# The upper parts of the weights, rounded by a second DMA from DRAM instead of by ScalarE

## The chip, the cores and the metric

One core of a Trainium2 chip runs the whole kernel. The metric is the time of one execution on the device in microseconds. Before the change it is 1176.87 us in the median of three runs (1175.96 to 1178.97).

## What is computed

One layer of a decoder for 512 prompt tokens and 8 sample tokens (520 columns in all), width 1024, float32. Cut to what matters here:

```python
z = rms_norm(x) @ w_in                       # 1024 -> q | k | v | g | gMLP u | gMLP v | a_ret | a_gm
o, new_state = retention(q, k, v, state)     # 4 heads, key 256, value 512; 8 samples with their own states
A = (silu(g) * head_rms(o)) @ w_ret_o
B = (gelu(u) * (tril(W_s) @ layer_norm(gelu(v)) + b)) @ w_gm_o
h = x + (sigmoid(a_ret) * A + sigmoid(a_gm) * B) @ w_o
h = h + (silu(f_gate) * f_up) @ w_ffn_down   # f_gate, f_up = rms_norm(h) @ w_ffn_in, hidden 2816
y = rms_norm(h)
```

The states of the samples (8 samples, 4 heads, 512 KB each) are read, updated and written back.

## The kernel before, in words

Activations lie with features on the partitions and tokens in the free dimension. A product of float32 quality is made of three products in float32r, a shorter float type: every operand is split into an upper part (the value rounded to float32r) and a lower part (what the rounding leaves), and `product` (L99 to L108) adds upper x upper, upper x lower and lower x upper for each 128x128 weight tile and each half of the 520 tokens. A block of weights is eight such tiles, [128, 1024] or 512 KB: 48 matmuls with 260 columns. There are 178 blocks: 80 of `w_in`, 16 of `w_ret_o`, 8 of `w_gm_o`, 8 of `w_o`, 44 of `w_ffn_in` and 24 of `w_ffn_down` (eight of these have six tiles).

`weights` (L84 to L97) brings a block in. SP issues the load of the raw block (L95), ScalarE casts it into the upper part `whi`, and VectorE subtracts (raw - `whi`) into the lower part `wlo`; both are in `split` (L79 and L82). Three raw buffers and two each of `whi` and `wlo` go round. The first two blocks come in pieces (`cuts`), and the three blocks of the last output tile go into big buffers of their own (`keep`: `khi`, `klo`).

The order of the stages is: the first activations and their split; four heads, each with q, k, v and gate products, the scores, the outputs, and eight samples; then the gMLP branch, the merge, the hidden layer and the output with its norm. Within a head `sample` loads a state S (three buffers, SP, L433), gets a broadcast of q and k from DRAM for every two samples (`qkb`, POOL, L436), has ScalarE make the key-value products (L442), updates S on VectorE (L443), stores it (`out_rss`, POOL, L444) and reads it out on VectorE (L447). At the end of a head come its row sums (`stats`, L511 and after) and the gated output (`gated`, L520), which are worked off in the next head's time and feed `gate_out`.

POOL also makes the rotary sums (L275, L276), the gate products (L515, L602), the layer norm's scale and shift (L595, L596) and the product in the hidden layer (L721).

Every engine works through its own queue in order, and so do the DMA issues in the queues of SP and POOL. That order is not written out by hand: a planner simulates the program and puts each instruction into its engine's queue when its inputs and a buffer are free in the simulation; semaphores hold the order on the chip.

Of the kernel before, what the change touches and what calls it, by code (L numbers as in the profile page):

```python
# [13 lines left out]
P = 128  # L14
D = 1024          # model width
KT = D // P       # contraction tiles of the model width
NP = 512          # prompt tokens
NS = 8            # sample tokens
T = NP + NS       # all tokens, in the free dimension
HT = T // 2       # tokens of one matmul  # L20
H = 4             # retention heads
DK = 256
DV = 512
NC = 4            # chunks of 128 prompt tokens
G = 4             # gMLP groups
NF = 2816 // P    # feature tiles of the hidden layer
PAST = 4096
EPS = 1e-6

NBIG = 26         # [128, 2, 520] buffers that all phases share  # L30
NFP = 4           # more of them, once the first phases' own buffers are free
NTMP = 5          # [128, 520] buffers for what lives shortly
NWARM = 16        # matmuls before the first operands
NSP = 6           # tiles of the first activations that GpSimd squares

# [6 lines left out]
def step_kernel(ctx: ExitStack, tc: tile.TileContext, io):  # L42
# [10 lines left out]

# [1 line left out]
    def ttile(name):  # L55
# [20 lines left out]
    def split(hi, lo, src, hi_eng=None, lo_eng=None):  # L76
        """src = hi + lo exactly, both with 12 significant bits."""
        if hi_eng is None:
            nc.scalar.copy(out=hi, in_=src)  # L79
        else:  # L80
            hi_eng.tensor_copy(out=hi, in_=src)
        (lo_eng or nc.vector).tensor_tensor(out=lo, in0=src, in1=hi.bitcast(F32), op=ALU.subtract)  # L82

    def weights(src, n, cuts=(), keep=False):  # L84
        """A block of n 128x128 weight tiles, split into two parts (in pieces, where it must start early)."""
        raw = wp.tile([P, 8 * P], F32, name="wraw", tag="wraw", bufs=3)
        if keep:
            hi, lo = flat(wide("khi", F32R)), flat(wide("klo", F32R))
        else:
            hi = wp.tile([P, 8 * P], F32R, name="whi", tag="whi")  # L90
            lo = wp.tile([P, 8 * P], F32R, name="wlo", tag="wlo")
        at = [0, *cuts, n]
        for a, b in zip(at, at[1:]):
            sl = slice(a * P, b * P)
            nc.sync.dma_start(out=raw[:, sl], in_=src[:, sl])  # L95
            split(hi[:, sl], lo[:, sl], raw[:, sl])
        return hi, lo  # L97

    def product(ps, w, at, x, first, last, fs=(0, 1)):  # L99
        """ps += w[:, at].T @ x, as hi*hi + hi*lo + lo*hi."""  # L100
        sl = slice(at * P, (at + 1) * P)
        wh, wl = w[0][:, sl], w[1][:, sl]
        for n, (a, k) in enumerate(((wh, 0), (wh, 1), (wl, 0))):
            for f in fs:
                nc.tensor.matmul(  # L105
                    (ps[f] if isinstance(ps, list) else ps[:, f])[:, 0:HT], a, x[:, k, f * HT : (f + 1) * HT],
                    start=first and n == 0, stop=last and n == 2,
                )  # L108

    def small_rsqrt(v, n, parts=P):  # L110
        """v ** -0.5 of a few positive columns: a bit-level guess and Newton's steps."""
        i0 = small.tile([P, 16], I32, name="rs_i0")[:parts, 0:n]
# [14 lines left out]
    def rsqrt_table(after):  # L127
        """Has ScalarE load the table of the roots ahead of their time, but after this."""
        one = small.tile([P, 1], F32, name="one", bufs=1)
        nc.scalar.activation(out=one, in_=after[:, 0:1], func=AF.Abs_reciprocal_sqrt)  # L130

    def newton_rstd(out, ps, scale, n):
        """(ps * scale + eps) ** -0.5"""
        y, v, t = (stile(f"rr_{x}")[:, 0:n] for x in "yvt")
        nc.vector.tensor_scalar(out=v, in0=ps, scalar1=scale, scalar2=EPS, op0=ALU.mult, op1=ALU.add)
        nc.scalar.activation(out=y, in_=v, func=AF.Abs_reciprocal_sqrt)
        nc.vector.scalar_tensor_tensor(out=t, in0=y, scalar=-0.5, in1=y, op0=ALU.mult, op1=ALU.mult)
        nc.vector.tensor_tensor(out=t, in0=t, in1=v, op=ALU.mult)
        nc.vector.scalar_tensor_tensor(out=out, in0=t, scalar=1.5, in1=y, op0=ALU.add, op1=ALU.mult)

    def row_rstd(out, ps, width):
        """The same of sums over features, all tokens."""
        y, v, t = (stile(f"rr_{x}") for x in "yvt")
# [11 lines left out]
    def add_square(acc, src, first, pool=False, add=None):  # L155
        """acc (+)= src ** 2, the sums over features on their way."""
        q = acc if first else stile("sqr")
# [7 lines left out]
    def row_sums(acc):  # L165
        """Sums over the partitions, in all partitions, in two banks."""
        pr = [stile(f"sq{x}", F32R) for x in "hl"]
# [11 lines left out]
    def scaled_split(pr, src, g):  # L179
        """src * g (per partition) in two parts."""  # L180
        nc.scalar.activation(out=pr[:, 0, :], in_=src, func=AF.Copy, scale=g)
# [3 lines left out]

# [1 line left out]
    ones_r = const.tile([P, P], F32R, name="ones_r")  # L187
# [30 lines left out]

    # keeps TensorE's clock up until the first operands are there
    warm = ttile("warm")[:, 0:HT].bitcast(F32R)  # L220
# [29 lines left out]

    br = []           # what becomes the merge: retention branch, two feature tiles each

# [1 line left out]
    def unscaled(base, name):  # L254
        """The first two tiles, before the norm's scale is known."""
        raw = wide(f"{name}raw")
# [5 lines left out]
    def rotated(base, name, raw=None):  # L262
        """Rotary on two feature tiles (one head): float32 [P, 2, T]."""
        def turns(i, src):
# [14 lines left out]
    def gate_out(h, gated):  # L279
        """This head's part of the retention branch's output projection."""  # L280
        for m2 in range(KT // 2):
# [13 lines left out]
    def head(h, prev, dec):  # L295
# [24 lines left out]

        # keys by token, with the decay to the end of the prompt
        kth, ktl = wide("kth", F32R), wide("ktl", F32R)
# [21 lines left out]

        # scores, transposed: [s, t >= s]; rows of 512, 384 | 256 + 128
        sch = wide("sch", F32R), wide("sch2", F32R)
# [18 lines left out]

        # values by token
        vt = [wide(f"vt{i}", F32R) for i in range(4)]  # (hi, lo) x two chunks each
        vs = small.tile([P, NC, NS], F32, name="vs", bufs=2)

# [27 lines left out]

        # the samples' queries and keys, broadcast over the partitions by way of DRAM
        ps = aux("ps_qk")
# [14 lines left out]

        # swish gate
        gts = []
# [9 lines left out]

        # the samples: new states and what is read of them, values over the partitions
        os_ = small.tile([P, NC, NS], F32, name="os_", bufs=2)
# [22 lines left out]

        # the output by feature
        of = [wide("of0"), wide("of1")]
# [12 lines left out]

        # the state after the prompt
        def last_state():
# [33 lines left out]

        # the head norm and the gate, for the next head's time
        class Gating:
# [27 lines left out]

# [1 line left out]
    def sig_gate(m, name, out):  # L534
        """out = sigmoid of a merge gate, one feature tile."""
        pa = z_tile(m, name)
# [3 lines left out]
    def gmlp(gp):  # L540
# [40 lines left out]

        # layer norm over the features, by token
        def layer_norm(v, parts):
# [19 lines left out]

        # what the values of a chunk mix to, by feature
        mixed = [wide(f"mix{i}") for i in range(KT // 2)]
# [50 lines left out]

# [1 line left out]
    sg = [wide(f"sg{i}") for i in range(KT // 2)]  # L658
# [33 lines left out]

# [1 line left out]
    def ffn_tile(m, name):  # L694
# [9 lines left out]
    for i in range(NF):  # L704
        a, b = ttile("fa"), ttile("fb")
        pg = ev(ffn_tile(i, "ps_fg"))
        if i == 0:
            # the norm's scale isn't known yet
            nc.scalar.copy(out=halves(a), in_=pg)
# [16 lines left out]
    def down_weights(i, keep=False):  # L726
        """The three blocks of a tile of the output projection: (weights, first tile, tiles)."""
        for k0 in range(0, NF, 8):
# [8 lines left out]
    rsqrt_table(a)  # L737
    # the residual sum, times the last norm's gain
    hn = []
# [8 lines left out]

    # the last feature tile, half of the tokens after half of them
    i = KT - 1  # L750
# [97 lines left out]
```

## Time and profile before

| what | before |
|---|---|
| median of three runs | 1176.87 us |
| span of the profiled execution (its first to its last instruction) | 1173.5 us |
| TensorE matmul busy | 1146.2 us, 98% |
| VectorE busy | 682.5 us, 58% |
| ScalarE busy | 435.6 us, 37% |
| GpSimd busy | 231.5 us, 20% |
| moved by DMA | 148.49 MB, mean 127 GB/s |

The profile is of one execution. PE is TensorE's matmul, PEld its weight load, DVE is VectorE, ACT ScalarE, POOL GpSimd; SP only issues DMAs. A q behind an engine's name is its instruction queue. Issuing a DMA does not count as busy. A row with an arrow names the tile written and the tiles read. Waits are inferred: "A <- B: 3.6, 1, 3.6" is A idle for 3.6 us in total, once, 3.6 us at the longest, until B.

### The profile page before, as it was taken

The numbers are of one execution on the slowest core, as the hardware profiler recorded it, in microseconds if no ns is written. First come the engines' busy times: TensorE is split into PE (matmuls) and PEld (weight loads), VectorE is DVE, ScalarE is ACT, GpSimd is POOL, SyncE is SP. The second block draws the span as 40 slices with busy tenths as digits, with TensorE's granted clock in tenths as the row PEclk, the third lists the DMA queues.
The fourth block names the chain that finished last, engine by engine and source line by source line (L and its number), as shares of the span: only waits on it lengthen the run. The fifth ranks groups of instructions, "written<-read, shape, count | busy, mean of one in ns | idle before, by whom it ended". The sixth has DMA issues, their size and how long they took to land.

```text
span 1173.5 us, 21664 instructions
## 1 busy us (share of the span) xinstructions
PE 1146.2 (98%) x9240; PEld 1128.9 (96%) x9240; DVE 682.5 (58%) x1063; ACT 435.6 (37%) x672; POOL 231.5 (20%) x183
## 2 busy tenths in 40 slices
PE   8999999999999999998999999999999999999995
PEld 7999999999999998998999999999999999999995
DVE  7788747874896588449744336445445454532233
ACT  4355355532644365223233333333222222232220
POOL 7213201310141013007522012211101010101101
PEclk9999999999999999999799999999999999999998
DMA  7267337632753284221123222522222323223322
GB/s 268 88 216 282 105 114 251 233 121 90 268 200 127 90 295 168 78 91 55 58 73 100 96 90 94 160 91 90 90 91 90 102 82 105 86 87 99 83 80 73
DMA packets 45056, 148.49 MB, mean 127 GB/s; under 512 B 5240, under 2 KB 7688, under 8 KB 44960
## 3 DMA queue, kind: packets, MB, share of 16 engines
q1 hardware_dynamic: 37280, 119.74, 31.3%
q0 software_dynamic: 7680, 27.38, 6.2%
q8 instruction: 72, 1.18, 0.4%
q14 instruction: 24, 0.20, 0.1%
HBM read 125.99 MB, written 21.10 MB: 125 GB/s over the span
## 4 chain that ended last, share of the span: by engine, by line
PE 76%; DVE 12%; DMA 4%; issue 3%; ACT 3%; POOL 0%; DVEq 0%; ACTq 0%; POOLq 0%; SPq 0%
PE ps_fu L105 11%; PE ps_fg L105 11%; PE ps_fd L105 10%; PE ps_ro L105 8%; PE ps_v L105 5%; PE ps_gm L105 4%; PE ps_gu L105 4%; PE ps_ag L105 4%; PE ps_wo L105 4%; PE ps_gv L105 4%; DVE wlo L82 2%; DMA S<-in_st 2%; PE ps_g L105 2%; PE k L105 2%; PE ps_ar L105 2%
## 5 line engine op out<-in xcount | busy, mean ns | idle before, releaser
L79 ACT CAST whi<-wraw 128x1024 fp32r<-128x1024 f32 (+2 forms) x180 | 184.9, 1027 | 475.0 <-issue 96.5
L82 DVE TENSOR_TENSOR wlo<-wraw,whi 128x1024 fp32r<-128x1024 f32 (+2 forms) x180 | 256.9, 1428 | 97.0 <-ACT whi L79 92.3
L105 PE MATMUL ps_fu<-hg,whi 128*128 128x260 f32 x704 | 113.3, 283 | 0.0
L105 PE MATMUL ps_fg<-hg,whi 128*128 128x260 f32 x704 | 113.3, 283 | 0.0
L105 PE MATMUL ps_fd<-act,whi 128*128 128x260 f32 x616 | 98.7, 282 | 0.0
L105 PEld LDWEIGHTS ps_fu<-hg,whi 128*128 128x128 f32 x704 | 96.6, 189 | 0.0
L105 PEld LDWEIGHTS ps_fg<-hg,whi 128*128 128x128 f32 x704 | 96.6, 188 | 0.0
L105 PEld LDWEIGHTS ps_fd<-act,whi 128*128 128x128 f32 x616 | 84.3, 188 | 0.0
L105 PE MATMUL ps_g<-xg,whi 128*128 128x260 f32 x512 | 82.7, 283 | 0.0
L105 PE MATMUL ps_ro<-gated,whi 128*128 128x260 f32 x512 | 82.3, 282 | 0.0
L105 PE MATMUL ps_v<-xg,whi 128*128 128x260 f32 x512 | 82.2, 282 | 0.0
L721 POOL TENSOR_TENSOR fa<-fa,fb 128x520 f32<-128x520 f32 x22 | 28.7, 1304 | 229.1 <-ACT whi L79 194.2
L105 PEld LDWEIGHTS ps_ro<-gated,whi 128*128 128x128 f32 x512 | 70.6, 188 | 0.5
L105 PE MATMUL ps_fg<-hg,wlo 128*128 128x260 f32 x352 | 70.7, 282 | 0.0
L105 PE MATMUL ps_fu<-hg,wlo 128*128 128x260 f32 x352 | 70.7, 282 | 0.0
L105 PEld LDWEIGHTS ps_v<-xg,whi 128*128 128x128 f32 x512 | 70.1, 188 | 0.0
L105 PEld LDWEIGHTS ps_g<-xg,whi 128*128 128x128 f32 x512 | 69.9, 188 | 0.0
L442 ACT ACTIVATE kv<-qkb,vs 128x256 f32<-128x256 f32 x128 | 54.0, 498 | 26.7 <-DMA qkb<-qks 22.5
L105 PE MATMUL ps_fd<-act,wlo 128*128 128x260 f32 x308 | 61.9, 282 | 0.0
L720 DVE TENSOR_TENSOR fb<-ps_fu,rstd 128x520 f32<-128x520 f32 x21 | 14.7, 700 | 76.8 <-PE ps_fu L105 76.8
L163 POOL TENSOR_TENSOR sq<-sq,sqr 128x520 f32<-128x520 f32 x19 | 33.0, 1734 | 132.7 <-ACT sqr L161 128.4
L447 DVE SCALAR_TENSOR_TENSOR junk<-S,qkb 128x256 f32<-128x256 f32 x128 | 53.9, 421 | 2.3
(245 smaller groups left out, 2552.3 us busy)
## 6 DMA issues: line engine op xcount, KB each, us to landing
wraw<-in_w_in SPq DMA_DIRECT2D x78, 512.0 KB, 3.5
wraw<-in_w_ffn_in SPq DMA_DIRECT2D x44, 512.0 KB, 3.5
S<-in_st SPq DMA_DIRECT2D x32, 512.0 KB, 4.6
out_rss<-S POOLq DMA_DIRECT2D x32, 512.0 KB, 5.1
qkb<-qks POOLq DMA_DIRECT2D x16, 512.0 KB, 5.0
wraw<-in_w_ret_o SPq DMA_DIRECT2D x16, 512.0 KB, 3.5
wraw<-in_w_ffn_down SPq DMA_DIRECT2D x16, 512.0 KB, 3.5
wraw<-in_w_gm_o SPq DMA_DIRECT2D x8, 512.0 KB, 3.5
```

The lines of the kernel that those rows point to most:

```text
L79: nc.scalar.copy(out=hi, in_=src)
L82: (lo_eng or nc.vector).tensor_tensor(out=lo, in0=src, in1=hi.bitcast(F32), op=ALU.subtract)
L105: nc.tensor.matmul((ps[f] if isinstance(ps, list) else ps[:, f])[:, 0:HT], a, x[:, k, f * HT : (f + 1) * HT], start=first and n == 0, stop ...
L163: (add or nc.gpsimd).tensor_tensor(out=acc, in0=acc, in1=q, op=ALU.add)
L442: nc.scalar.activation(out=kv[:, j, :], in_=kb, func=AF.Copy, scale=vs[:, j, b : b + 1])
L447: nc.vector.scalar_tensor_tensor(out=junk, in0=S[:, j, :], scalar=1.0, in1=qb, op0=ALU.mult, op1=ALU.mult, accum_out=os_[:, j, b : b + 1],)
L720: nc.vector.tensor_tensor(out=halves(b), in0=pu, in1=halves(rstd), op=ALU.mult)
L721: nc.gpsimd.tensor_tensor(out=a, in0=a, in1=b, op=ALU.mult)
```

## The change

`weights` loads a block twice. POOL issues a DMA from DRAM straight into `whi`, whose type is float32r, so that the transfer rounds; SP loads the raw block as before; VectorE subtracts as before. ScalarE's cast is gone, save in the two blocks with `cuts`. The raw buffers become two, the buffers of `whi` three; `wlo` keeps two.

```diff
     def weights(src, n, cuts=(), keep=False):
-        raw = wp.tile([P, 8 * P], F32, name="wraw", tag="wraw", bufs=3)
+        raw = wp.tile([P, 8 * P], F32, name="wraw", tag="wraw", bufs=2)
         if keep:
             hi, lo = flat(wide("khi", F32R)), flat(wide("klo", F32R))
         else:
-            hi = wp.tile([P, 8 * P], F32R, name="whi", tag="whi")
+            hi = wp.tile([P, 8 * P], F32R, name="whi", tag="whi", bufs=3)
             lo = wp.tile([P, 8 * P], F32R, name="wlo", tag="wlo")
         at = [0, *cuts, n]
         for a, b in zip(at, at[1:]):
             sl = slice(a * P, b * P)
+            if cuts:
+                nc.sync.dma_start(out=raw[:, sl], in_=src[:, sl])
+                split(hi[:, sl], lo[:, sl], raw[:, sl])
+                continue
+
+            nc.gpsimd.dma_start(out=hi[:, sl], in_=src[:, sl])
             nc.sync.dma_start(out=raw[:, sl], in_=src[:, sl])
-            split(hi[:, sl], lo[:, sl], raw[:, sl])
+            nc.vector.tensor_tensor(out=lo[:, sl], in0=raw[:, sl], in1=hi[:, sl].bitcast(F32), op=ALU.subtract)
         return hi, lo
```

The rest of the diff takes comments out.

## Rows read from the trace of the kernel before

**Rows 1.** The page: the span, then busy us, share and instructions of each engine.
```profile
span 1173.5 us, 21664 instructions
...
PE 1146.2 (98%) x9240; PEld 1128.9 (96%) x9240; DVE 682.5 (58%) x1063; ACT 435.6 (37%) x672; POOL 231.5 (20%) x183
```

**Rows 2.** TensorE's waits: us in total, times, longest.
```profile
PE ps_ar L105 <- DVE mv L588: 3.6, 1, 3.6
...
PE ps_mix L620 <- DVE gvl L82: 1.8, 1, 1.8
PE ps_ss L173 <- ACT sqh L79: 1.6, 1, 1.6
...
PE ps_ar L105 <- DVE ve L590: 1.4, 1, 1.4
...
PE ps_v L105 <- DVE wlo L82: 0.7, 2, 0.4
```

**Rows 3.** Windows: first and last head's sample stretch; busy us, count, clock, DMA share.
```profile
72.00:104.00 32.00, 32.00 (x233) 30.40 (x232) 26.65 (x73) 20.30 (x40) 5.34 (x10) 1.00 0.88 307
...
409.00:441.00 32.00, 32.00 (x238) 30.70 (x238) 26.62 (x75) 19.77 (x39) 5.35 (x10) 1.00 0.82 293
```

**Rows 4.** Chain of waits, second and fourth head: start us, us, what.
```profile
195.19 5.74 DMA out_rss<-S
...
200.99 8.36 DMA S<-in_st
...
237.63 2.44 DVE gt L520 x4
240.07 1.15 DVE wlo L82
...
241.26 0.86 PE ps_v L105 x5
...
405.52 1.06 ACT whi L79
```

**Rows 5.** Chain of waits in the hidden layer.
```profile
842.32 5.76 PE ps_fu L105 x48
```

**Rows 6.** Line 79, ScalarE: duration in ns (min, median, max), first and last start.
```profile
L79 ACT CAST whi<-wraw x180: 388/1052/1061, 3.0 to 1133.9; 128x1024 fp32r<-128x1024 f32 x168, 128x768 fp32r<-128x768 f32 x7, 128x512 fp32r<-128x512 f32 x3, 128x256 fp32r<-128x256 f32 x2
...
L79 ACT CAST khi<-wraw x3: 840/1049/1055, 1128.6 to 1134.9; 128x1024 fp32r<-128x1024 f32 x2, 128x768 fp32r<-128x768 f32 x1
```

**Rows 7.** Timeline of VectorE and ScalarE, hidden layer: start us, us, what, idle before.
```profile
848.12 0.70 DVE L720 TENSOR_TENSOR fb<-ps_fu,rstd 128x520 f32<-128x520 f32 x1 [3.69 <-PE ps_fu L105]
849.00 2.37 DVE L82 TENSOR_TENSOR wlo<-wraw,whi 128x1024 fp32r<-128x1024 f32 x1 [0.18 <-ACT whi L79]
...
847.92 1.05 ACT L79 CAST whi<-wraw 128x1024 fp32r<-128x1024 f32 x1 [4.19 <-PE ps_fu L105]
```

**Rows 8.** Windows of `whi` alone (PE, PEld, DVE, ACT): the first sample stretch.
```profile
72.00:104.00 32.00, 16.44 (x105) 14.07 (x104) 4.86 (x4) 4.15 (x4) 1.00 0.88 307
```

**Rows 9.** DMA queues: packets, MB, share of 16 engines' span (q1 SP, q0 POOL).
```profile
q1 hardware_dynamic: 37280, 119.74, 31.3%
q0 software_dynamic: 7680, 27.38, 6.2%
```

**Rows 10.** DMA issues: count, KB each, median us from issue to landing.
```profile
wraw<-in_w_in SPq DMA_DIRECT2D x78, 512.0 KB, 3.5
...
S<-in_st SPq DMA_DIRECT2D x32, 512.0 KB, 4.6
out_rss<-S POOLq DMA_DIRECT2D x32, 512.0 KB, 5.1
...
out_rsp<-sf POOLq DMA_DIRECT2D x4, 512.0 KB, 3.2
```

**Rows 11.** Timeline of POOL in the second head's sample stretch.
```profile
210.99 0.53 POOL L444 DMA_DIRECT2D out_rss<-S  x1 [8.65 <-DVE S L443]
```

**Rows 12.** Windows: the gMLP stretch (PE, PEld, DVE, ACT, POOL, clock, DMA).
```profile
520.00:570.00 50.00, 43.23 (x310) 42.06 (x309) 45.47 (x97) 12.64 (x17) 29.92 (x14) 0.83 0.20 65
```

## The prediction

> **What bounds the kernel now.** I first read the busy shares and the slices of the page. TensorE is busy for 98% of the span, ScalarE for 37%, GpSimd for 20% [rows 1]. So the removed work sits on an engine with spare time, and what there is to gain is the 27.3 us that TensorE is not busy (1173.5 - 1146.2). Next, TensorE's waits say where they are: 6.8 us in three waits of the gMLP stretch (3.6 + 1.8 + 1.4), 1.6 us at a row sum, 0.7 us in front of value products that wait for a lower part [rows 2]. What is left lies at the start and at the very end, which no block that changes reaches. Last, the windows and the chain of waits show the tight place. Each of the four heads has a stretch of 32 to 33 us in which eight samples pass: a state is loaded, updated, stored and its buffer loaded again. The 16 DMA engines are 82 to 88% busy there (first and last of four rows) [rows 3], and the chain runs through its transfers: a store takes 5.74 us and the load behind it 8.36 us. It then ends on TensorE: at 237.63 us VectorE multiplies the head's gates, subtracts a lower part behind them, and TensorE takes that block up at once at 241.26 [rows 4]. TensorE waits only 0.3 us there (0.7 in two such places [rows 2]), but it does wait: what makes the samples later makes TensorE later.
>
> From the hidden layer on, TensorE takes a block of 48 products every 5.76 us without a gap [rows 5], which is 0.120 us a product.
>
> **What is removed.** The row of the casts has 180, five of which (256 or 512 wide) are the pieces of the first two blocks and stay; the three into the kept blocks go too: 178 of 1.05 us, eight of them narrower, about 185 us of ScalarE [rows 6]. In the second half they are hidden: ScalarE casts a block at 847.92, VectorE's subtraction ends at 851.37, and TensorE needs the block only 5.76 us after the buffers came free [rows 5, 7]. In the sample stretch four casts leave per head [rows 8], of which the chain holds one (at 405.52 us, 1.06 us) [rows 4]. I credit 1.0 us a head.
>
> **What is added.** 178 transfers of 512 KB (eight of them 384 KB), together 92.3 MB more. What 16 engines pay follows from the queue rows: 31.3% of 1173.5 us for 119.74 MB is 3.07 us a MB, 6.2% for 27.38 MB is 2.66 [rows 9]. So one transfer of 0.524 MB occupies them for 1.39 to 1.61 us, and the mean share goes from 38% to about 60%. No row shows a transfer that rounds. The nearest are POOL's plain ones, which land 3.2 to 5.1 us after issue [rows 10]. I take 5.1.
>
> In the sample stretch four more transfers are 5.6 to 6.4 us of DMA. The engines are idle there for 3.8 us (12% of 32) to 5.8 us (18%) [rows 3], so at best nearly all of it fits into gaps and costs 0, and at worst the chain pays 6.4 us. The chain's transfers already queue: 8.36 us for a load whose median is 4.6 [rows 4, 10]. So I take two thirds of 6, 4.0 us. Less the 1.0 of the cast this is +3 us a head. TensorE waited at the end of three of the four (for the lower part after the first and the second head, 0.7 us together, for the row sum after the last, 1.6 us) [rows 2, 4], so these have no slack. For the third I assume 2 us. Sum: 3 x 3 + 1 = **+10 us**.
>
> **What is moved.** Each new issue takes about 0.53 us of POOL's queue, as the sample stores do [rows 11]: 94 us in all, on an engine that is busy for 231.5. It waits until TensorE has left the block three back, and behind it on POOL stand the sample stores, the broadcasts of q and k, the rotary sums and the gate products. The other way round it stands behind stores that wait for VectorE, up to 8.65 us at 210.99 us [rows 11]. In the stretch a block comes every 8 us (four in 32), so two blocks ahead is 16 us; less 0.5 for the issue, 5.1 to 8.4 for landing and 1.2 for the subtraction, 6 to 9 us are left. That is the length of this wait, so this cover is thin: 0 in the sum, up to 2.7 us twice a head in the range (+22).
>
> In the second half the upper part is issued when block n ends, and the subtraction for block n+3 may run from the end of n+1. VectorE has 0.9 us in front of it and takes up to 2.37 [rows 7]. TensorE wants n+3 two blocks after n ended. Landing may therefore take 11.52 - 0.53 - 0.9 - 2.37 = 7.7 us before it waits; by the rows it takes 3.2 to 5.1. Cost 0. The raw buffers go from three to two: SP then waits for the subtraction two blocks back, and the state loads and the token loads stand behind it. A raw block lands in 3.5 us [rows 10], within one block of 5.76. Also 0.
>
> In the gMLP stretch POOL is busy for 29.9 of 50 us and VectorE for 45.5 [rows 12]. Eight more issues are 4.3 us in POOL's queue, in front of the products that VectorE waits for. Against this stand subtractions that no longer wait for a cast. I take **+1 us**, with -5 and +8 as ends. At the start one 1.4 us transfer may come in front of the first activations: 0, at most 1.4.
>
> Sum: 1173.5 + 10 + 1 = 1184.5 us for a profiled execution. Its span is 3.4 us below the runs' median (1176.87), so **1188 us**.
>
> **Rivals.** *Hidden anyway.* The planner puts the transfers into the gaps and the end of each head has slack: within 0.3% of before (1173.3 to 1180.4), about 1177. For it: ScalarE's relief, two blocks of lead. Against: three heads with no slack.
>
> *Faster.* The upper part is there before the lower part's buffer comes free, so every subtraction can start 1.05 us earlier. Place: the gMLP stretch, where VectorE decides. There TensorE idles 6.8 us and runs slower afterwards: 310 products take 43.2 us, at 0.120 us they would take 37.2; the granted clock is 0.83 in the mean, so part of it is at the lower of the two levels (1.2 GHz) [rows 12]. With the 2.3 us of the heads up to 15 us can be had; it decides once the subtractions of that stretch come over a microsecond earlier. I price it at 6 us: 1171. Against: VectorE hardly waits for casts there, and POOL, which gets the issues, is part of the same chain.
>
> *Queue in front of the stores.* The new transfers stand in POOL's own DMA queue, in front of the stores and broadcasts on which the next load waits. One in front costs 1.39 us, and twice that while SP's queue moves as well, 2.8. Four a head are 11 us in place of 4: 3 x 10 + 8 + 1 = +39, 1216. It speaks for this that all 16 sample broadcasts and 32 stores are issued there [rows 10].
> The Trainium skill, on the page "DMA: Bandwidth & Descriptors", section "Queues, rings and completion order", says that each DMA engine goes round the queues that have work, packet by packet, and takes one queue's descriptors in ring order. By that rule the result would be this rival's rather than mine; the 8.36 us load right behind a store fits either.
>
> *Rounding transfers are slow.* From 7.7 us of landing on, the three upper buffers set the pace: each block is late by a third of what is over. At 10 us that is 0.77 us for each of the hundred blocks after the gMLP stretch (16 of `w_in`, 8 + 8 + 44 + 24), +77, with the heads about 1265 or more. No row speaks for or against the price.
>
> That the transfer doesn't round but copies would leave every instruction in its place, and the time with it; it has no case of its own.
>
> **Chances.** Forecast (1181 to 1205) 0.36, queue in front 0.10, slow transfers 0.12, hidden 0.22, faster 0.20. A change under 0.3% can't be told from none here. So slower 0.58, same 0.22, faster 0.20. The range leaves out the slow transfers and the far end of faster: 1170 to 1235.
>
> **What would show it.** The product blocks after the gMLP stretch stay at 5.76 us with no wait for a lower part; POOL's queue shows issues of about 0.53 us; new transfers land within 7.7 us; the DMA share of the four stretches goes over 0.9 and each gets longer by 3 us or more; TensorE's waits for lower parts or row sums at the ends of heads grow to about 10 us in all. I am wrong if these stretches keep their length, if TensorE waits in the second half, or if the gMLP stretch moves by more than 5 us either way.

## The result and the profile after

The changed kernel takes 1190.85 us in the median of four runs (1182.98 to 1195.75), the kernel before 1177.17 in the four beside it (1175.96 to 1178.97): 1.0113 times as long, with a 95% interval of 1.0077 to 1.0150. The forecast was 1188. The profiled execution has a span of 1187.0 us, 13.5 more than before.

The page of the kernel after, the rows that answer to [rows 1] and [rows 9]. (The POOL figure, before and after, does count DMA issues, which stand in the trace with a duration: 178 new ones at 0.55 us.)

```profile
span 1187.0 us, 21732 instructions
...
PE 1152.3 (97%) x9240; PEld 1135.9 (96%) x9240; DVE 650.0 (55%) x1063; ACT 261.0 (22%) x494; POOL 338.7 (29%) x361
...
q0 software_dynamic: 33312, 119.66, 31.7%
q1 hardware_dynamic: 37280, 119.74, 30.1%
```

ScalarE's busy time falls by 174.6 us (435.6 - 261.0; about 185 were to go), and the kernel gains nothing by it. (The blocks listed ahead add up to 180, of which 178 now come by the new transfer.) POOL's queue takes 31.7% x 1187.0 / 119.66 = 3.14 us a MB, SP's 30.1% x 1187.0 / 119.74 = 2.98. So the rounding transfer costs about as much as a plain one. The DMA issues of the page after, with the median from issue to landing in the last column, say the same [rows 10]:

```profile
wraw<-in_w_in SPq DMA_DIRECT2D x78, 512.0 KB, 4.6
whi<-in_w_in POOLq DMA_DIRECT2D x78, 512.0 KB, 3.9
...
S<-in_st SPq DMA_DIRECT2D x32, 512.0 KB, 6.6
out_rss<-S POOLq DMA_DIRECT2D x32, 512.0 KB, 5.8
```

The rounded part lands in 3.9 us; a raw block now takes 4.6 instead of 3.5, a state 6.6 instead of 4.6. The chain of waits in the hidden layer of the kernel after shows that the second half isn't slowed [rows 5]:

```profile
902.35 5.74 PE ps_fu L111 x48
```

TensorE's waits of the kernel after (us in total, times, longest) against [rows 2]:

```profile
PE q L111 <- DVE xg L188: 4.2, 3, 3.1
PE ps_ar L111 <- DVE sa L543: 3.6, 1, 3.6
PE ps_ss L179 <- ACT sqh L79: 3.0, 2, 2.8
PE ps_mix L626 <- DVE gvl L82: 2.8, 1, 2.8
PE k L111 <- DVE wlo L102: 1.8, 2, 1.5
```

Three places: the start (q waits for the first activations), the ends of the heads (k and the row sum `ps_ss`), the gMLP stretch (`ps_ar`, `ps_mix`). Waits alone don't tell the whole loss, because after a wait the granted clock falls too. The first 60 us of the kernel after, columns as in [rows 3]:

```profile
0.00:60.00 60.00, 52.47 (x366) 51.24 (x367) 38.57 (x45) 15.36 (x24) 27.92 (x28) 0.89 0.67 226
```

and of the kernel before:

```profile
0.00:60.00 60.00, 54.57 (x399) 51.70 (x400) 44.99 (x53) 25.40 (x39) 29.47 (x23) 0.97 0.52 179
```

TensorE gets 366 products done instead of 399, at a mean granted clock of 0.89 instead of 0.97: a larger part of the stretch at the lower of the two levels (1.2 and 2.4 GHz). Of the 4.0 us that 33 products take, 2.1 are idle time (54.57 - 52.47); the rest is that products take longer.

To locate the loss I number the 9240 matmuls in the order of time and compare when the same number starts, in the profiled execution of each kernel and of the kernel before. (The planner's order differs from that of before at 385 numbers at most.) The 4350th lies inside the gMLP stretch, the 4650th behind it. All runs of the next section stand here, with the time by which the product comes later (us):

| kernel | 150th | 750th | 900th (end of head 1) | 2250th | 3600th (end of head 4) | 4200th | 4350th | 4650th (behind gMLP) | 9150th |
|---|---|---|---|---|---|---|---|---|---|
| after | 4.2 | 5.1 | 8.2 | 7.1 | 9.2 | 9.3 | 4.4 | 14.0 | 13.4 |
| e1 second load by SP | 0.4 | 2.6 | 2.9 | 2.1 | 3.5 | 3.5 | 2.5 | 5.6 | 5.7 |
| e1b second load by GpSimd | 3.4 | 4.9 | 5.4 | 10.3 | 14.8 | 14.9 | 13.1 | 14.3 | 15.4 |
| e2 start by ScalarE | 0.1 | 0.3 | 5.9 | 4.5 | 6.8 | 6.9 | 2.0 | 16.0 | 15.4 |
| e3 gMLP by ScalarE | 3.6 | 4.7 | 12.6 | 10.9 | 11.7 | 11.7 | 11.6 | 14.7 | 14.2 |
| e4 both by ScalarE | -0.5 | 0.2 | 7.2 | 5.9 | 8.5 | 8.5 | 7.2 | 8.7 | 8.2 |
| e5 before + 4 KB store | 4.2 | 4.2 | 4.4 | 3.7 | 5.7 | 5.7 | 4.8 | 4.8 | 4.8 |
| e6 second half only | 0.0 | -0.1 | 1.0 | -0.4 | 0.3 | 0.3 | -2.4 | -0.6 | -1.0 |
| e7 other Newton steps | 0.9 | 0.9 | 2.0 | 1.0 | 3.0 | 3.0 | -7.9 | -1.2 | -1.2 |
| e9 both by ScalarE, stores by ScalarE | -1.1 | -0.9 | 3.6 | 3.6 | 8.2 | 8.2 | 5.5 | 7.2 | 6.8 |
| e9b before, stores by ScalarE | 0.8 | 0.8 | 2.3 | 1.3 | 2.5 | 2.4 | 1.5 | 4.6 | 4.6 |

One execution each, and a kernel's executions differ by some microseconds (the ranges below): the ones shown of e1b, e2 and e9b are the slowest of their kernels, those of e4 and e6 the fastest. So steps of 3 us and more are read here, not single ones, and even these with care: e3 has the same edit in the heads as the kernel after and loses 7.9 us at the first end, where that loses 3.1. The kernel after loses 4 to 5 us at the start, reaches 9.3 by the end of the heads, loses 4.7 in the gMLP stretch and gets 0.6 back in the second half, where a block takes 5.74 us and not 5.76.

**The start.** VectorE's timeline of the kernel after (start us, us):

```profile
12.81 6.20 DVE L82 TENSOR_TENSOR wlo<-wraw,whi 128x512 fp32r<-128x512 f32 x1
```

and GpSimd's:

```profile
12.29 0.59 POOL L100 DMA_DIRECT2D whi<-in_w_in  x1
12.90 2.07 POOL L165 TENSOR_TENSOR sqr<-xt 128x520 f32<-128x520 f32 x2
14.92 1.30 POOL L169 TENSOR_TENSOR sq<-sq,sqr 128x520 f32<-128x520 f32 x1
16.18 1.04 POOL L165 TENSOR_TENSOR sqr<-xt 128x520 f32<-128x520 f32 x1
17.19 1.27 POOL L169 TENSOR_TENSOR sq<-sq,sqr 128x520 f32<-128x520 f32 x1
```

Before, the same places read, on VectorE and on GpSimd:

```profile
12.14 1.54 DVE L82 TENSOR_TENSOR wlo<-wraw,whi 128x512 fp32r<-128x512 f32 x1
```

```profile
11.63 1.50 POOL L159 TENSOR_TENSOR sqr<-xt 128x520 f32<-128x520 f32 x1
```

Before, the two engines take turns, and each instruction lasts 1.5 to 1.8 us. After, from the DMA issue at 12.29 on, five GpSimd instructions run one behind the other at 1.04 to 1.30 us, and VectorE's subtraction, 1.54 us before, lasts 6.20 and ends at 19.01, just behind the last of them. The Trainium skill, page "SBUF — State Buffer", section "Who interferes with whom", says that a VectorE instruction with two SBUF inputs contends with a GpSimd instruction that reads SBUF, and that the order of issue decides which of the two is held up. The trace of before agrees, with its instructions in turns; that five pass while one waits is this trace's.

**The gMLP stretch.** The same again; the VectorE row, and the GpSimd rows beside it:

```profile
584.36 6.52 DVE L82 TENSOR_TENSOR gvl<-gvt,gvh 128x1024 fp32r<-128x1024 f32 x1
```

```profile
583.68 0.59 POOL L100 DMA_DIRECT2D whi<-in_w_in  x1
584.29 1.31 POOL L608 TENSOR_TENSOR br<-br,sa 128x520 f32<-128x520 f32 x1
585.55 0.57 POOL L100 DMA_DIRECT2D whi<-in_w_in  x1
586.15 2.40 POOL L602 TENSOR_TENSOR gvt<-gvt,lnb 128x1024 f32<-128x1024 f32 x1
588.49 1.29 POOL L608 TENSOR_TENSOR br<-br,sa 128x520 f32<-128x520 f32 x1
```

`gvl` takes 1.22 us when nothing is in its way (575.63 in the trace of before). The 2.8 us wait of `ps_mix` is for `gvl`; it was 1.8 before, and it is 2.5 and 2.9 in e4 and e3, where this subtraction isn't held up. So the wait alone doesn't tell what the 6.52 us cost.

The net loss of 4.7 us hides two opposite parts. Windows from the 4275th to the 4350th product and on to the 4575th, of the kernel before:

```profile
557.50:574.60 17.10, 15.30 (x77) 15.01 (x77) 12.64 (x19) 1.83 (x3) 11.20 (x6) 0.55 0.19 63
574.60:601.10 26.50, 26.50 (x228) 26.41 (x227) 15.29 (x29) 6.90 (x9) 7.67 (x4) 1.00 0.17 61
```

and of the kernel after:

```profile
566.90:579.00 12.10, 11.47 (x78) 11.26 (x77) 11.86 (x16) 0.64 (x1) 9.55 (x7) 0.79 0.31 91
579.00:615.10 36.10, 33.25 (x228) 32.81 (x227) 21.07 (x32) 6.12 (x7) 13.04 (x10) 0.81 0.31 103
```

First 5.0 us are won: TensorE is back at the higher level sooner (a mean clock of 0.79 instead of 0.55). Then 9.6 are lost: 2.85 us of idle time, and products at a mean clock of 0.81 instead of 1.00. By the table e2, with the same edit in this stretch, wins 4.9 us up to the 4350th and loses 14.0 behind it; the other kernels but e7 win 0.1 to 2.7 and lose 0 to 3.1. So the rounding transfers seem to do both here. Why the clock came back sooner stays open.

**The heads.** The chain of waits of the kernel after, end of the first head:

```profile
92.70 7.23 DMA S<-in_st
...
103.81 8.85 DMA S<-in_st
...
120.63 2.28 DVE wlo L102
...
122.96 1.23 PE k L111 x8
```

This is the mechanism forecast: state loads behind other transfers, late samples, then a lower part for which TensorE waits. How late the samples are, and how full the DMA engines, is read from windows that go from the first to the last store of a head, as GpSimd issues them; of the kernel before:

```profile
72.13:102.21 30.08, 30.08 (x220) 28.66 (x219) 24.73 (x71) 19.08 (x38) 4.80 (x9) 1.00 0.87 300
183.34:215.03 31.69, 31.69 (x235) 30.33 (x234) 24.94 (x71) 19.02 (x38) 4.81 (x9) 1.00 0.82 289
296.96:328.28 31.32, 31.32 (x232) 30.05 (x232) 25.05 (x71) 19.12 (x38) 4.82 (x9) 1.00 0.85 294
409.59:439.94 30.35, 30.35 (x229) 29.27 (x228) 24.97 (x71) 19.14 (x38) 4.81 (x9) 1.00 0.82 297
```

and of the kernel after:

```profile
79.00:114.30 35.30, 35.30 (x263) 33.85 (x263) 27.50 (x74) 18.30 (x39) 7.17 (x14) 1.00 0.96 331
191.08:224.55 33.47, 33.47 (x244) 31.86 (x243) 27.41 (x75) 18.30 (x39) 6.94 (x13) 1.00 0.96 341
304.17:337.02 32.85, 32.85 (x239) 31.25 (x239) 27.38 (x75) 17.80 (x38) 6.95 (x13) 1.00 0.93 318
416.73:450.88 34.15, 34.15 (x249) 32.57 (x248) 27.56 (x75) 18.38 (x39) 6.96 (x14) 1.00 0.95 329
```

The stretches are longer by 5.2, 1.8, 1.5 and 3.8 us, 12.3 in all, and denser: the DMA share is 0.93 to 0.96 instead of 0.82 to 0.87. VectorE isn't slowed there: in the first one no subtraction of a block and no update of a state lasts over 1.23 us in either kernel. The last stores come 12.1, 9.5, 8.7 and 10.9 us later. TensorE itself is 5.1 us late ahead of the first end (750th product) and 7 to 7.6 ahead of the others, so relative to it the samples lose 7, 2, 2 and 4. TensorE loses 3.1 us at the first end, nothing to speak of at the second and third, and 2.2 at the last.

### The profile page after: what moved, and what is told of

Same layout as the page of the kernel before. It is cut to its first block, busy times and chain, and to the rows that moved or that the text cites. A ratio compares the mean times of both kernels' runs of the same rounds, so it can differ in the third digit from the quotient of the medians.

```text
span 1187.0 us, 21732 instructions
## 1 busy us (share of the span) xinstructions
PE 1152.3 (97%) x9240; PEld 1135.9 (96%) x9240; DVE 650.0 (55%) x1063; ACT 261.0 (22%) x494; POOL 338.7 (29%) x361
## 3 DMA queue, kind: packets, MB, share of 16 engines
q0 software_dynamic: 33312, 119.66, 31.7%
q1 hardware_dynamic: 37280, 119.74, 30.1%
## 4 chain that ended last, share of the span: by engine, by line
PE 78%; DVE 11%; DMA 6%; issue 2%; ACT 1%; POOL 1%; SPq 0%; DVEq 0%; POOLq 0%; ACTq 0%
PE ps_fg L111 11%; PE ps_fu L111 11%; PE ps_fd L111 10%; PE ps_ro L111 8%; PE ps_v L111 6%; DMA S<-in_st 4%; PE ps_gu L111 4%; PE ps_gm L111 4%; PE ps_wo L111 4%; PE ps_ag L111 4%; PE ps_gv L111 3%; PE k L111 3%; PE ps_g L111 2%; DVE wlo L102 2%; PE q L111 2%
## 5 line engine op out<-in xcount | busy, mean ns | idle before, releaser
L102 DVE TENSOR_TENSOR wlo<-wraw,whi 128x1024 fp32r<-128x1024 f32 (+1 forms) x175 | 220.3, 1259 | 86.1 <-PE ps_fd L111 37.7
L100 POOL DMA_DIRECT2D whi<-in_w_in x78 | 42.9, 551 | 229.7 <-PE ps_ro L111 46.6
L100 POOL DMA_DIRECT2D whi<-in_w_ffn_in x44 | 24.6, 559 | 171.8 <-PE ps_fu L111 102.1
L726 DVE TENSOR_TENSOR fb<-ps_fu,rstd 128x520 f32<-128x520 f32 x21 | 14.7, 700 | 80.3 <-PE ps_fu L111 80.3
L111 PEld LDWEIGHTS ps_fu<-hg,wlo 128*128 128x128 f32 x352 | 54.1, 188 | 0.0
```

Of the source, the lines that this page charges most:

```text
L100: nc.gpsimd.dma_start(out=hi[:, sl], in_=src[:, sl])
L102: nc.vector.tensor_tensor(out=lo[:, sl], in0=raw[:, sl], in1=hi[:, sl].bitcast(F32), op=ALU.subtract)
L111: nc.tensor.matmul((ps[f] if isinstance(ps, list) else ps[:, f])[:, 0:HT], a, x[:, k, f * HT : (f + 1) * HT], start=first and n == 0, stop ...
L726: nc.vector.tensor_tensor(out=halves(b), in0=pu, in1=halves(rstd), op=ALU.mult)
```

## The experiments

The theory of the forecast: four more transfers in each sample stretch make the samples late (*bytes*). After reading the trace there were two more: the new DMA issues on GpSimd let its next instructions pass in front of VectorE (*starved VectorE*); and the transfers suffer from, or hold up, what shares GpSimd's queue (*GpSimd's queue*).

**Second load by SP.** From the kernel after; ScalarE rounds, but from a second raw copy in a buffer of its own. Against the kernel before, the bytes are new, and little else. (Raw buffers 2 in place of 3, `whi` 2.)

```diff
-            nc.gpsimd.dma_start(out=hi[:, sl], in_=src[:, sl])
+            nc.sync.dma_start(out=raw2[:, sl], in_=src[:, sl])
             nc.sync.dma_start(out=raw[:, sl], in_=src[:, sl])
+            nc.scalar.copy(out=hi[:, sl], in_=raw2[:, sl])
```

> ScalarE rounds again, but from a second raw copy (one buffer) that SP loads beside the first: the bytes of the change, no new issue on POOL. Theory S (a DMA issue on POOL close to POOL's own tensor operations makes VectorE sit through all of them, 6.20 us at 12.81 us and 6.52 us at 584.36 us of the changed kernel): both jumps, at the start (+4.2 to 5) and in the gMLP stretch (+4.7), are gone, 1177 to 1182 us, no VectorE operation over 4 us. Theory B (the doubled traffic, my prediction's): the sample stretches stay longer and it remains at 1185 or more.

1180.46 us (1177.95 to 1187.0) against 1177.39; 1.0022 (1.0007 to 1.0038). The bytes, loaded this way, are worth some 3 us, a quarter of the loss. In the table they come in at about 2.6 by the 750th product, 1 in the heads, 2 in the gMLP stretch. The first sample stretch, from its first to its last store:

```profile
72.82:106.50 33.68, 33.68 (x246) 32.09 (x246) 26.36 (x74) 22.27 (x43) 4.79 (x9) 1.00 0.95 340
```

It is as full as in the kernel after. The four stretches are 3.6, 0.7, 2.7 and 1.8 us longer than before, 8.8 in all: most of the 12.3, with SP as issuer. Yet TensorE loses 0.9 us in the heads (2.6 to 3.5), so they have some slack.

**Second load by GpSimd.** The same, with that plain load issued by GpSimd.

```diff
-            nc.sync.dma_start(out=raw2[:, sl], in_=src[:, sl])
+            nc.gpsimd.dma_start(out=raw2[:, sl], in_=src[:, sl])
```

> The same, only that POOL issues the second load (plain, no rounding). Theory S: VectorE operations of 4 us or more come back where POOL also computes, 4 to 10 us over the version with SP's loads, about 1183 to 1192. Theory B: the same as with SP's loads within 2 us, since the bytes are the same. If the rounding itself costs, this one stays clearly under the changed kernel's 1190.9.

1187.74 us (1183.57 to 1193.22); 1.0082 (1.0056 to 1.0109). The same bytes, the same casts, another issuer: some 7 us more than by SP (1187.74 - 1180.46), and an interval that overlaps that of the kernel after. So a plain load can cost about as much, with GpSimd as the issuer. That the kernel after pays for the same reason isn't shown, for the places differ: this kernel loses 0.5 us at the first head's end and 9.4 in the other heads, and nothing in the gMLP stretch. I had looked for VectorE instructions of 4 us and over, and there are none in this trace; at the start GpSimd's first square waits 4.2 us for the activations' load instead of 2.1. The rest shows as waits for lower parts:

```profile
PE ps_v L112 <- DVE wlo L103: 5.6, 4, 1.9
PE ps_ar L112 <- DVE wlo L103: 5.1, 2, 3.1
```

With its one second raw buffer a load can't be issued until ScalarE has left that buffer, which may add to this. So the run says what GpSimd as issuer costs here, not by which way.

**4 KB at the start.** The kernel before, plus one store of eight columns, issued by GpSimd where the kernel after has its first rounding transfer. Its data are of no use.

```diff
+        if note is not None:
+            nc.gpsimd.dma_start(out=note, in_=q[:, 0:8])
...
-        add_square(sq, xs[kt], kt == 0, pool=kt < NSP)
+        add_square(sq, xs[kt], kt == 0, pool=kt < NSP, note=tiny if kt == 2 else None)
```

> The kernel before, with one DMA more: POOL stores eight columns (4 KB) of a square of the first activations to a scratch in DRAM; it stands in POOL's queue where the first rounding transfer of the changed kernel stands, between the squares. Theory S (the issue itself makes VectorE sit through POOL's following operations): a VectorE operation of 4 to 6.5 us at 11 to 14 us, TensorE's 450th product 4 to 5 us later, 1181 to 1182 in all. Rival (the 512 KB, or the wait for them in VectorE's queue, did it): nothing over 2 us at the start, 1177.

1180.0 us (1179.55 to 1182.2) against 1177.17; 1.0032 (1.0019 to 1.0044). VectorE's row and GpSimd's rows in this kernel:

```profile
12.51 6.17 DVE L82 TENSOR_TENSOR wlo<-wraw,whi 128x512 fp32r<-128x512 f32 x1
```

```profile
11.96 0.59 POOL L163 DMA_DIRECT2D tiny<-sqr  x1
12.56 2.07 POOL L159 TENSOR_TENSOR sqr<-xt 128x520 f32<-128x520 f32 x2
```

6.17 us against 6.20: 4 KB do what 512 KB do. At the start the loss is the issue itself, in front of a row of GpSimd instructions, and neither bytes nor rounding. This settles that one instruction, 4.2 us at the 150th product, and 2.8 us in the median (1181 to 1182 were expected).

**Start by ScalarE, gMLP stretch by ScalarE, both.** From the kernel after: the blocks of the first six calls (two of these are the ones in pieces), the 20 of the gMLP stretch, or both, are cast by ScalarE as before.

```diff
+        by_act = bool(cuts) or blocks_cast["left"] > 0 or blocks_cast["stage"]
+        blocks_cast["left"] -= 1
...
-            if cuts:
+            if by_act:
```

> The changed kernel, but the first six blocks (q, k and the first two values of the first head) are cast by ScalarE. Theory S: the start's jump goes, TensorE's 600th product comes at 87 us instead of 91.4, the time falls by 4 to 5 us to about 1186; the gMLP jump stays. Theory B: six of 178 transfers are gone, the start is worth 1 us, about 1190.

> The changed kernel, but ScalarE casts the blocks of the gMLP stretch before the gMLP u products (8 gMLP v, 8 a_ret, 4 of the last head's output). Theory S: the 6.5 us VectorE operation there is gone and with it 4 to 6 us, about 1185 to 1187; the start's jump stays. Theory B: the stretch has a DMA share of 0.2 to 0.3, nothing to win there, 1190 or more.

> The changed kernel with the first six blocks and the 20 blocks of the gMLP stretch cast by ScalarE: no rounding transfer where POOL computes without a pause. Theory S: no VectorE operation over 4 us; what remains over the kernel before is what the sample stretches cost, 3 to 8 us, mostly at the end of the first head: 1180 to 1185. Theory B: 1188 or more.

Start: 1185.76 us (1180.23 to 1190.66), 1.0067 (1.0043 to 1.0092); about 1186 was expected. gMLP stretch: 1189.54 (1185.96 to 1194.79), 1.0095 (1.0070 to 1.0121), where I had expected 1185 to 1187: a miss. Both: 1188.17 (1186.77 to 1191.23), 1.0105 (1.0089 to 1.0121), where I had expected 1180 to 1185: a miss. In the traces each edit does its work: with the start undone the loss there is 0.1 us, with the stretch undone the 6.5 us instruction is gone (though the stretch still costs 3.0), with both no VectorE instruction lasts over 4 us and the stretch costs 0.2 instead of 4.7. Yet with both undone the time hardly falls, and none of these three intervals lies wholly under that of the kernel after. The table offers a reason for the start: with it the first head's end is 7.2 us late (both undone) and 5.9 (start undone), without 8.2. The last store of that head comes at 111.43 us in the kernel with both undone (114.30 after, 102.21 before), so the samples, not the start, set when the head ends there. Most of a gain at the start is then waited away:

```profile
PE k L115 <- issue: 3.0, 1, 3.0
...
PE k L115 <- DVE wlo L106: 1.7, 2, 1.4
```

Behind such a wait the clock falls as well: 0.95 in the mean from 60 to 130 us in this kernel, 1.00 in the kernel before. (The row names no releaser for the 3.0 us.) This is read from single executions, and the median with the start alone undone, 5 us under that of the kernel after, speaks against it; it isn't shown.

**Second half only.** From the kernel after: ScalarE casts all blocks ahead of the gMLP's u products, and the remaining 100 come by rounding transfers.

```diff
-            if cuts:
+            if by_scalar[0]:
```

> Rounding transfers only from the gMLP u products on (100 blocks); the 78 before are cast by ScalarE, with two raw and three upper buffers. All theories: TensorE never waits there, so within 2 us of the kernel before (1175 to 1179). If it is slower by more than 3 us, the buffers (two raw in place of three) cost something in the first half.

1178.6 us (1174.43 to 1183.8), 1.0021 (1.0006 to 1.0036), inside the 1175 to 1179 expected. Its profiled execution, the fastest of its twelve, ends 0.9 us earlier than before's. In its trace the second half is free, as the forecast has it, and the other numbers of buffers, which this kernel keeps, cost nothing that one sees. The median's 0.2% has no place in this trace.

**Stores by ScalarE.** From the kernel with both undone, and as a control from the kernel before: the samples' stores go to ScalarE's queue.

```diff
-            nc.gpsimd.dma_start(out=io["rss"][b, h].rearrange("p (j d) -> p j d", j=NC), in_=S)
+            nc.scalar.dma_start(out=io["rss"][b, h].rearrange("p (j d) -> p j d", j=NC), in_=S)
```

> The kernel e4_start_and_gmlp_by_scalar (rounding transfers in the heads and from the merge on), with one more edit: the 32 stores of the sample states are issued by ScalarE instead of GpSimd, so that they no longer share an instruction queue and a DMA queue with the rounding transfers. Theory Q (what the heads lose is lost because the rounding transfers share GpSimd's queue and DMA queue with the stores and broadcasts of the samples; the bytes alone are worth the 2 to 4 us that e1_second_load_by_sp showed there): against its control e9b the products after the last head begin 1 to 4 us later, and the first head's end at most 3 us later; the time is 0.1 to 0.5% over the control's. Theory B (the 16 DMA engines are full in the sample stretches, whoever issues): the first head's end stays 5 to 8 us later and the last head's 7 to 9 us, as in e4_start_and_gmlp_by_scalar; the time is 0.7 to 1.1% over the control's. By both the second half costs nothing.

> The control of e9_stores_by_scalar: the kernel before with the 32 stores of the sample states issued by ScalarE instead of GpSimd, and nothing else. Both theories: within 0.4% of the kernel before (1172 to 1182), since TensorE hardly waits at the ends of the heads there; ScalarE may stand behind a store that waits for VectorE, up to some microseconds a head, which would show as later casts in the heads.

1184.23 us (1181.4 to 1189.85), the control 1176.38 (1173.85 to 1179.81): 0.67% over it, between the two forecasts. By the table's measure, from the 750th product to the first head's end the kernel loses 3.0 us to its control (-1.7 to +1.3), where the one with both undone lost 7.0 to the kernel before (0.2 to 7.2). By the end of the last head it is 7.4 (-1.7 to +5.7) against 8.3 (0.2 to 8.5). In the medians the loss is two thirds of that with both undone (0.67% over the control, against 1.05% over the kernel before). So sharing GpSimd's queue with the stores may explain part of the loss, and it does not explain the heads as a whole.

The broadcasts of q and k share GpSimd's queue too, and no run moves them. What the traces have on them is the first head's first broadcast, up to the product that waits for it, in the chains of the kernel before, of the one with the second load by SP, of the kernel after and of the one with both undone:

```profile
60.38 4.07 DMA qkb<-qks
...
58.33 4.15 DMA qkb<-qks
...
67.70 6.04 DMA qkb<-qks
...
62.65 8.43 DMA qkb<-qks
```

In the last two GpSimd issues it right behind a rounding transfer (at 67.15 and 61.48 us). The longer it takes, the more the first head's end loses, on the whole: 0.3 us by SP, 3.1 after, 7.0 with both undone; 5.6 in e2 (6.79) and 7.9 in e3 (8.27); 1.1 in e6 (4.05), which has no rounding transfers there. So this queue is the likeliest reason for the first head; that it is the cause isn't shown.

**Newton steps with a scalar operand.** The trace of before showed one-column VectorE instructions of up to 2.3 us in the gMLP stretch. If two inputs from SBUF are what makes them wait for GpSimd, another form frees them. From the kernel before; for two [128, 1] inputs one becomes a per-partition scalar:

```diff
-            nc.vector.scalar_tensor_tensor(out=t, in0=y, scalar=-0.5, in1=y, op0=ALU.mult, op1=ALU.mult)
-            nc.vector.tensor_tensor(out=t, in0=t, in1=v, op=ALU.mult)
-            nc.vector.scalar_tensor_tensor(out=y, in0=t, scalar=1.5, in1=y, op0=ALU.add, op1=ALU.mult)
+            nc.vector.tensor_scalar(out=t, in0=y, scalar1=-0.5, scalar2=y, op0=ALU.mult, op1=ALU.mult)
+            nc.vector.tensor_scalar(out=t, in0=t, scalar1=v, scalar2=1.5, op0=ALU.mult, op1=ALU.add)
+            nc.vector.tensor_scalar(out=y, in0=t, scalar1=y, scalar2=None, op0=ALU.mult)
```

> The kernel before, with the Newton steps of the layer norm's root written with a per-partition scalar operand in place of a second tile (three operations a step as before). Theory S with its lock (VectorE waits for POOL only in operations with two tiles in SBUF): the one-column operations of 1.2 to 2.3 us beside POOL's fall to 0.1 to 0.2 us, 10 us or more of VectorE in the gMLP stretch, and TensorE wins back 3 to 10 us there: 1167 to 1174, faster than both kernels. Rival (they wait for POOL in any form): no change, 1177.

1173.66 us (1169.32 to 1174.65); 0.9966 (0.9953 to 0.9978): faster than both kernels, and inside the 1167 to 1174 expected. One of the three lines, before (ns: min, median, max):

```profile
L121 DVE SCALAR_TENSOR_TENSOR rs_y<-rs_t,rs_y x15: 138/153/2310, 533.3 to 567.2; 128x1 f32<-128x1 f32 x12, 8x1 f32<-8x1 f32 x3
```

and with the edit:

```profile
L121 DVE TENSOR_SCALAR rs_y<-rs_t,rs_y x15: 192/204/214, 537.0 to 564.1; 128x1 f32<-128x1 f32 x12, 8x1 f32<-8x1 f32 x3
```

The median is 51 ns dearer, the longest falls from 2310 to 214 ns, and the gMLP stretch becomes 4.2 us shorter (from +3.0 at the 4200th product to -1.2 at the 4650th; in kernels without rounding transfers there this step is -1.0 to +3.0). The two long ones, 2.3 us each, stand beside GpSimd products of 2.4 us. The Trainium skill says in the same section of "SBUF — State Buffer" that a VectorE instruction with at most one SBUF input, outside its two-port modes, doesn't contend with GpSimd. The 214 ns agree, though no run shows whether the new form is outside these modes.

## Why the prediction was right, and where it was not

- **Sum.** Forecast 1188.0, measured 1190.85. The profiled span was to grow by 11.0 and grew by 13.5. The parts are less good than the sum: a start priced at nothing and a gMLP stretch priced too low make up for heads priced too high.
- **Start, 0 (at most 1.4).** Mis-sized: 4 to 5 us. I had written that no block that changes reaches the start, and priced one transfer in front of the first activations; what costs is its issue on GpSimd, which leaves VectorE waiting through five instructions. Shown, by the 4 KB store.
- **Heads, +10.** Too much for this kernel: from the 750th to the 4200th product it loses 4.2 us (9.3 - 5.1). The kernels with one or both of the other places undone lose 6.6 to 8.3 there. "3 us a head" is 3.1 at the first end, nothing at the second and third, 2.2 at the last. For the second head "no slack" failed: the samples lose 2 us there and TensorE none. A wait of 0.3 us at a head's end was too small a sign of what is late next.
- **Its mechanism.** Right for the stretches themselves. The DMA share was to go over 0.9 in all four, and does (0.93 to 0.96); each was to become 3 us longer, and they become 5.2, 1.8, 1.5 and 3.8 longer, 12.3 in all for the 12 priced. The price of a MB, 3.14 us, lies just over the two bounds (2.66 and 3.07). The same bytes by SP make them 8.8 us longer. What failed is the step from there to TensorE: of the 12.3 us about 4 reach it, and of the 8.8 about 1. So bytes alone account for some 3 us over the whole run (second load by SP). What makes the heads cost more with GpSimd as issuer stays open: the stores' queue is not all of it, and the broadcasts, which fit the first head, stay untried.
- **gMLP stretch, +1 (-5 to +8).** Mis-sized: +4.7, inside the bounds, as the difference of 5 won and 9.6 lost. The place was right (GpSimd's issues among its products), the way probably wrong: not 4.3 us of GpSimd's queue, but one subtraction on VectorE that took 6.52 us, and a lower clock behind it. Without that subtraction the stretch cost 0.2 us in one kernel and 3.0 in another, so its share isn't settled.
- **Second half, 0.** Right: 5.74 us a block, no wait. Landing (3.9 us, and 3.8 in the hidden layer) was inside the 7.7 of cover; issues of 0.55 us as taken (0.53).
- **Waits at the ends of heads about 10 us in all.** Wrong: 4.8 (3.0 + 1.8) in the rows for row sums and lower parts.
- **Rivals.** *Hidden anyway* and *faster* are out by the interval. What the first says does happen in the second half, which costs nothing, and for two of the four heads. The second named the gMLP stretch, and there 5 us are won for a while; whether by earlier subtractions isn't shown. *Slow rounding transfers*: out, 3.9 us. *Queue in front of the stores*, priced at 11 us a head: not at that size. The stores land in 5.8 us instead of 5.1, and moving them away leaves most of the heads' loss. On a smaller scale it may hold for the first head's broadcasts.

What the forecast lacked was to be seen in the trace of before: a one-column VectorE instruction takes up to 2310 ns there beside GpSimd, against 153 in the median. I priced GpSimd's new instructions by what queues behind them on GpSimd, and not by what they do to VectorE beside it. And the agreement of 2.9 us is largely luck: errors of about 4 to 6 us in three places cancel, and the kernel's own runs spread over 12.8 us.

## What to carry to other kernels

Work moved to another engine isn't priced by its own duration alone, nor by the idle share of the engine it goes to: look at which engine shares something with it, and whether the path runs there. A loss that a trace shows at an early place may cost little when a later place has its own reason to be late: undo both before you add them up. Let a window follow the stretch that it is to show: from 72 to 104 us the kernel after has a DMA share of 0.86, from the first to the last store of the same head 0.96. For plain second loads from DRAM, try an issuer that computes nothing: here SP cost less than GpSimd.

## What the hardware showed that I had not expected

- A DMA issue of 0.59 us on GpSimd ended the alternation of GpSimd and VectorE: VectorE's next two-input instruction waited through the GpSimd instructions that followed, 6.20, 6.52 and, with a 4 KB store, 6.17 us. Not every issue does this: the kernel whose plain second loads GpSimd issues has no VectorE instruction of 4 us. Why VectorE isn't let in between these instructions stays open.
- The same plain second load, into one buffer, costs 0.22% when SP issues it and 0.82% when GpSimd does.
- A one-column VectorE instruction with two SBUF inputs took up to 2310 ns beside GpSimd; as an instruction with a per-partition scalar it never took more than 214.
